# Values stationary in attention's PV, two heads in the column halves, and an order that fills gaps, in a four-branch mixer layer on one core

## The chip, the core and the metric

The kernel runs on one core of one Trainium2 chip. Times are device microseconds (us) of that core. The kernel before has a median of 295.15 us over 3 runs (294.05 to 296.47); one further execution was taken with the profiler.

## What is computed

One layer of a sequence mixer on x (512 x 1024, f32). A single input projection `proj = x @ w_in` has 14 column groups of 256: queries, keys and values of two attentions (`qa ka va`, `qd kd vd`), the input of a state-space layer (`us`), three inputs of a gated recurrence (`qc fc ic`) and four gates (`g0` to `g3`). Four branches of width 256 follow:

```
ya = moba_attention(heads(qa), heads(ka), heads(va), rel_bias[:, :4])      # at this length: causal attention
yb = s5_mixer(us, ...)                                                      # state-space layer and GLU
yc = hgrn2_mixer(qc, fc, ic, lb)                                            # gated recurrence, in chunks of 64
yd = dilated_attention(heads(qd), heads(kd), heads(vd), rel_bias[:, 4:])    # causal, weighted by a multiplicity
y  = concatenate([ya, yb, yc, yd])
yg = y.reshape(..., 16, 64); yg = yg * rsqrt(mean(yg*yg) + eps)             # per 64 channels
y  = (yg * branch_gain * silu(gates)) @ w_out
x  = layer_norm(alpha * x + y) * ln_g + ln_b
```

Each attention has 4 heads of width 64; per head `softmax(q k^T / 8 + bias) v`. All is f32 accuracy: where f32 products go through the fast one-pass form (f32r), each factor is split into a high and a low part and three products are summed.

## The kernel before, in words

**Matmuls.** The projection is done per column group and half (`mm3`, line 291; `projections`, line 425): 8 pieces of the contraction by 3 products, each 128x128 weights against 512 moving columns (256 for the token-major groups `ic va vd`). The output projection (`omm`, line 1225) takes units (token tile i, column half c): 8 pieces k by 3 products of 512 columns. Six of the pieces are the partial part (`out_partial`), the last two need the second attention and are the final part (`out_final`). For the last unit alone the final part is cut into two runs of 256 columns, both into the one PSUM tile of the unit.

**Attention** goes by branch br (0 or 1), token tile i in the order 3, 2, 1, 0, and head. `attn_pair` (line 1111) computes the scores of two heads, one in rows 0 to 63 and one in rows 64 to 127 of the array (`sc`). `attn_head` (line 1125) adds the bias on DVE (`nl<-sc,TB`), takes the exponential on ACT, transposes the tile in pieces of 128x128 on PE (`pt<-ident,nl`), and copies it back (`pT<-pt`, on DVE for odd heads, on ACT for even ones). Then PV: for each key tile kt up to i, `po` (128 tokens x 64 columns) accumulates with P as the stationary operand and the values as the moving one, 64 columns at a time. After four heads `attn_norm` (line 1166) squares `po` on ACT (`sqa`), reduces on DVE, takes a power on POOL (`msa`), scales on DVE (`ya<-po,msa`), transposes on PE (`yt<-ident,ya`), applies gain and gate (`z`), and splits into `yh` and `yl`. One PSUM bank (tag `sm`) holds `po` until `ya` has been read from it.

**Recurrence.** `hgrn` (line 869) builds chunk scores in one diagonal step and three levels li = 0, 1, 2. A step is 32 f32 matmuls in quadrants of the array into four PSUM tiles of one bank each (`hs`, tags `sc` and `pt`); DVE merges them into `st`, by 8 multiplications with the identity for the diagonal, by 12 masked copies (`COPY_PREDICATED st<-cst,hs`) for a level.

**What sets the order.** All instructions come out of one planner (`Order`, line 128). Each part of the program is a generator that yields one operation, or a list of them for PE, or a wait. The planner holds a clock per engine, prices each operation by a table (`Op.cost`, line 57), and takes the first task by priority whose next operation may go: a PE operation only if what it needs is planned to be ready 1 us earlier, others if they do not leave the engine waiting. Buffers are counted as tokens (`sc` 2, `pt` 2, `pj` 3, `sm` 1, `raw` 4). Every engine then runs its instructions in the order that came out, and waits where a needed result is late. The input weights and the output weights pass through four `raw` buffers: a DMA brings a piece, ACT makes the high part (`woh<-wro`), DVE the low part (`wol<-wro,woh`), and this frees the buffer for the next DMA.

All records of compute instructions have line 207 of the kernel, in `trace`, so they are told apart by their tiles.

Of the kernel before, what the change touches and what calls it, by code (L numbers as in the profile page):

```python
# [11 lines left out]
F32 = mybir.dt.float32  # L12
# [21 lines left out]
NCP = 16  # L34
NW = 5
# [15 lines left out]
class Op:  # L51
# [5 lines left out]
    def cost(self):  # L57
# [6 lines left out]
        if e == "PE":  # L64
# [4 lines left out]
            if self.a[1].dtype == F32:  # L69
                if self.a[0].shape[0] == 64 and self.a[1].shape[0] == 64:  # L70
                    return (0.03 + n / 600) / 4
                return 2 * max(0.107, 0.013 + n / 1200)
            return 0.013 + n / 2400
        if e == "DVE":
# [8 lines left out]
            if f == "tensor_tensor_scan":  # L83
                return 0.42
            return 0.09 + m * 0.00107
# [41 lines left out]
class Order:  # L127
# [31 lines left out]

    def step(self, t):  # L160
# [20 lines left out]
        else:  # L181
# [62 lines left out]
def build(ctx: ExitStack, tc: tile.TileContext, xT, xN, w_in, w_out, ln_g, ln_b,  # L244
# [18 lines left out]
    def ps(nm, tag, shape=(128, 512)):  # L263
        return pp.tile(list(shape), F32, tag=tag, name=nm, bufs=dict(pj=NPJ, sm=4 - NPJ).get(tag, 2))
# [604 lines left out]
    def hgrn():  # L869
# [6 lines left out]
        def scores(pss, nm, shape, col):  # L876
            for a in range(2):
                for h in range(2):
                    pss[h, a] = ps(f"hs{nm}_{h}{a}", ("sc", "pt")[h], (128, 4, shape))
            ops = []  # L880
            for a in range(2):
                for c2 in range(4):
                    for h, cpar in ((0, 0), (1, 1), (0, 1), (1, 0)):
                        c = 2 * c2 + cpar
                        rh = slice(64 * h, 64 * h + 64)
                        d_, r = col(pss[h, a][64 * cpar:64 * cpar + 64, c2], rh, a, c)
# [3 lines left out]
        pss = {}  # L890
        yield Tok(sc=2, pt=2)
        yield from scores(pss, "d", 64, lambda d_, rh, a, c: (d_, qc[rh, a, 64 * c:64 * c + 64]))
        for h in range(2):
            for a in range(2):
                for q in range(2):
                    sl = slice(64 * q, 64 * q + 64)
                    yield V.tensor_tensor(st[h][sl, a], pss[h, a][sl],
                                          ident[sl, sl].unsqueeze(1).to_broadcast([64, 4, 64]), OP.mult)
# [14 lines left out]
        for li, m in enumerate((1, 4, 16)):  # L913
# [15 lines left out]
            pss = {}  # L929
# [12 lines left out]
            for h in range(2):  # L942
                for a in range(2):
                    dst = st[h][:, a].rearrange("p c (n s) -> p c n s", n=nn)
                    sr = pss[h, a].rearrange("p c (n s) -> p c n s", n=nn)
                    for d0, s0, n_, o_ in ((m, 0, 3, 0), (2 * m, 3 * m, 2, 48), (3 * m, 5 * m, 1, 80)):
                        mm = msk[:, li, o_:o_ + 16 * n_].rearrange("p (n s) -> p n s", n=nn)
                        yield V.copy_predicated(dst[:, :, :, d0:4 * m], mm.unsqueeze(1).to_broadcast([128, 4, nn, n_ * m]),
                                                sr[:, :, :, s0:s0 + n_ * m])
# [20 lines left out]
            tot = nt  # L970
        o.done("hgrn levels")
# [136 lines left out]
    SUM = small([128, 2, 4, 4], "ssum")  # L1108
# [304 lines left out]
```

## Time and profile before

| | |
|---|---|
| median of 3 runs | 295.15 us (294.05 to 296.47) |
| profiled execution | 296.08 us, of which the traced span is 294.3 us |
| PE busy | 282.3 us (96%) |
| DVE busy | 214.2 us (73%) |
| ACT busy | 140.1 us (48%) |
| POOL busy | 25.0 us (8%) |
| PE share of the chain that ended last | 82% |
| mean granted clock of TensorE | 0.991 |

The span runs from the first to the last instruction. A matmul's duration includes the way through the array, so that neighbouring records overlap; what one costs is the distance to the next start. An f32 matmul leaves two records, an f32r matmul and a transpose one each. The chain that ended last is followed back from the last instruction to whatever released it.

### The profile page before, as it was taken

What the parts mean: (1) busy time and instruction counts of PE and PEld (TensorE: products, weight loads), DVE (VectorE), ACT (ScalarE), POOL (GpSimd) and SP (SyncE); (2) the same over time, 40 slices, a digit from 0 to 9 for tenths busy, and PEclk for the clock granted to TensorE, in tenths of its full rate; (3) what the DMA queues carried; (4) which work ended last, traced back from release to release, by engine and by line L of the source; (5) the groups of instructions that cost most, each with busy time, mean ns of one, the idle gap of its engine ahead of it and who ended that gap; (6) DMA issues with size and microseconds to landing.
All of it is one profiled execution on the core that took longest, in us unless ns stands there. A gap on an engine that the chain in (4) does not pass through costs nothing.

```text
span 294.3 us, 5178 instructions
## 1 busy us (share of the span) xinstructions
PE 282.3 (96%) x1932; PEld 234.0 (80%) x1932; DVE 214.2 (73%) x529; ACT 140.1 (48%) x273; POOL 25.0 (8%) x30
## 2 busy tenths in 40 slices
PE   8999999999999999999999999999998999999980
PEld 3768789888899878688888898878987788888870
DVE  2876899999999699747976444566569844866655
ACT  4677561324443632178434796468677533111000
POOL 1100010000000001103001000100250011111201
PEclk9999999999999999999999999999999999999996
DMA  6956535513221999501211203542003880030011
GB/s 196 300 187 221 145 91 116 165 59 108 65 82 40 151 139 141 161 34 55 74 71 71 75 9 82 160 148 68 2 0 106 233 295 14 5 139 38 36 71 71
DMA packets 18741, 31.08 MB, mean 106 GB/s; under 512 B 2426, under 2 KB 5882, under 8 KB 18716
## 3 DMA queue, kind: packets, MB, share of 16 engines
q1 hardware_dynamic: 18716, 30.76, 37.6%
q8 instruction: 15, 0.25, 0.4%
q14 instruction: 10, 0.08, 0.1%
HBM read 27.27 MB, written 2.42 MB: 101 GB/s over the span
## 4 chain that ended last, share of the span: by engine, by line
PE 82%; DMA 7%; DVE 5%; ACT 2%; issue 2%; SPq 1%; DVEq 0%
PE pj_g L207 15%; PE out L207 14%; PE po L207 5%; PE pj_ic L207 4%; PE pj_va L207 4%; PE pj_qc L207 4%; DMA wro<-in_w_out_dram 4%; PE pj_ka L207 4%; PE pj_qa L207 4%; PE pj_us L207 4%; PE pj_vd L207 4%; PE sc L207 3%; PE pj_kd L207 3%; PE pt L207 2%; DMA wrus<-in_w_in_dram 2%; PE y L207 2%
## 5 line engine op out<-in xcount | busy, mean ns | idle before, releaser
L207 PE MATMUL pj_g<-xh,whg 128*128 128x512 f32 x64 | 26.3, 411 | 0.0
L207 PE MATMUL pj_g<-xh,wlg 128*128 128x512 f32 x64 | 25.0, 391 | 0.0
L207 PE MATMUL pj_g<-xl,whg 128*128 128x512 f32 x64 | 25.0, 390 | 0.0
L207 ACT ACT_TABLE_LOAD x18 | 23.1, 1283 | 1.0 <-PEq L1402 0.7
L207 ACT ACTIVATE nl<-nl,nm 128x512 f32<-128x512 f32 (+3 forms) x32 | 17.8, 557 | 8.3 <-DVE nm L207 8.2
L207 PE MATMUL out<-woh,yh 128*128 128x512 f32 x48 | 19.8, 413 | 0.0
L207 POOL TENSOR_TENSOR msa<-msa,mhalf 128x4 f32<-128x4 f32 x8 | 9.9, 1240 | 106.5 <-DVE msa L207 106.5
L207 PE MATMUL out<-woh,yl 128*128 128x512 f32 x48 | 18.9, 393 | 0.0
L207 ACT ACTIVATE whg<-wrg 128x512 fp32r<-128x512 f32 x16 | 10.1, 628 | 18.2 <-PE pj_g L207 12.3
L207 PE MATMUL out<-wol,yh 128*128 128x512 f32 x48 | 18.7, 390 | 0.0
L207 DVE TENSOR_TENSOR wlg<-wrg,whg 128x512 fp32r<-128x512 f32 x16 | 11.0, 686 | 8.4 <-ACT whg L207 8.3
L207 DVE CUSTOM_DVE_ANT_0 nl<-sc,TB 128x512 f32<-128x512 f32 (+3 forms) x32 | 15.0, 486 | 2.4 <-PE pt L207 1.6
L207 PEld LDWEIGHTS pj_g<-xh,whg 128*128 128x128 f32 x64 | 12.0, 188 | 3.7 <-issue 1.2
L207 ACT ACTIVATE yh<-z 128x256 fp32r<-128x256 f32 (+1 forms) x12 | 5.8, 487 | 18.0 <-DVE z L207 17.9
L207 PEld LDWEIGHTS pj_g<-xh,wlg 128*128 128x128 f32 x64 | 12.0, 188 | 2.7
L207 PE MATMUL pt<-ident,nl 128*128 128x128 f32 x80 | 13.4, 276 | 0.3 <-ACT pT L207 0.3
L207 PEld LDWEIGHTS pj_g<-xl,whg 128*128 128x128 f32 x64 | 12.0, 188 | 2.1
L207 DVE COPY_PREDICATED st<-cst,hs 128x192 f32<-128x192 int32 (+2 forms) x36 | 11.8, 354 | 0.7 <-PE hs L207 0.2
L207 DVE COPY pT<-pt 128x512 f32<-128x512 f32 (+3 forms) x16 | 7.7, 486 | 6.1 <-PE pt L207 6.0
L207 ACT ACTIVATE pT<-pt 128x512 f32<-128x512 f32 (+3 forms) x16 | 6.9, 430 | 10.1 <-PE pt L207 10.1
L207 PEld LDWEIGHTS pt<-ident,nl 128*128 128x128 f32 x80 | 9.8, 146 | 2.0 <-ACT pT L207 0.7
L207 PEld LDWEIGHTS po<-vd,pT 128*128 128x128 f32 x80 | 10.1, 191 | 1.6 <-DVE pT L207 0.6
(309 smaller groups left out, 829.0 us busy)
## 6 DMA issues: line engine op xcount, KB each, us to landing
wrg<-in_w_in_dram SPq DMA_DIRECT2D x16, 256.0 KB, 4.2
wro<-in_w_out_dram SPq DMA_DIRECT2D x16, 256.0 KB, 3.0
xr<-in_xT_dram SPq DMA_DIRECT2D x8, 256.0 KB, 4.5
TB<-scr SPq DMA_DIRECT2D x8, 256.0 KB, 10.6
xn<-in_xN_dram SPq DMA_DIRECT2D x4, 512.0 KB, 9.1
out_dram<-xn SPq DMA_DIRECT2D x7, 256.0 KB, 2.0
raw<-in_w_in_dram SPq DMA_DIRECT2D x8, 128.0 KB, 4.5
wrus<-in_w_in_dram SPq DMA_DIRECT2D x4, 256.0 KB, 5.0
```

The lines of the kernel that those rows point to most:

```text
L207: getattr(self.engines[op.eng], op.name)(*op.a, **op.k)
```

## The change

Six things are changed.

- PV has the values as the stationary operand (128 x 64) and P as the moving one (128 columns). The two heads of a pair write PSUM partitions 0 to 63 and 64 to 127, alternately. A pair's PV is a task of its own that starts when both P are there (`attn_pv`).
- The result is then channel-major. `attn_norm` copies it to SBUF on ACT, transposes it back on PE with two 128x128 transposes into the other half of the same bank, and goes on as before.
- The planner gets `earlier`: before it places an operation on ACT, DVE or POOL that would leave this engine waiting, it looks for another task's operation that fits into the gap. Attention's tasks get priority 6.5 (10 before; the output weights' splits have 8). The price table is changed for f32 matmuls with 64 output partitions and for masked copies.
- The recurrence's scores go into two tiles of two banks each, so that one DVE instruction merges what two did.
- The last unit of the output projection becomes two units of 256 columns each, with a PSUM tile each.
- The PSUM pool of the recurrence is closed after its levels, and the pool of `sc` and `pt` opened in its place.

```diff
+FIT = 0.5
@@ class Op: cost
+                if self.a[0].shape[0] == 64:
+                    return 0.013 + n / 1200
                 return 2 * max(0.107, 0.013 + n / 1200)
...
+            if f == "copy_predicated":
+                return 0.24 + m * 0.00095
             return 0.09 + m * 0.00107
@@ class Order
+    def earlier(self, t, e):
+        for t2 in self.tasks:
+            if t2 is t:
+                continue
+            while isinstance(self.fetch(t2), Wait) and all(n in self.events for n in t2["next"].names):
+                self.step(t2)
+            x = t2["next"]
+            x = x[0] if isinstance(x, list) else x
+            if isinstance(x, Op) and x.eng == e and max(t2["chain"], self.clk[e]) + FIT * x.cost() < t["chain"]:
+                return t2
+        return None
...
+            if e not in ("PE", "SP") and t["chain"] > self.clk[e] + 0.1:
+                t2 = self.earlier(t, e)
+                if t2 is not None:
+                    return self.step(t2)
@@ def hgrn
-            for a in range(2):
-                for h in range(2):
-                    pss[h, a] = ps(f"hs{nm}_{h}{a}", ("sc", "pt")[h], (128, 4, shape))
+            for h in range(2):
+                pss.append(four["hp"].tile([128, 2, 4, 128], F32, tag=f"hs{h}", name=f"hs{nm}_{h}", bufs=1))
...
-                for a in range(2):
-                    dst = st[h][:, a].rearrange("p c (n s) -> p c n s", n=nn)
...
+                dst = st[h].rearrange("p a c (n s) -> p (a c) n s", n=nn)
...
+                    yield V.copy_predicated(dst[:, :, :, d0:4 * m], mm.unsqueeze(1).to_broadcast([128, 8, nn, n_ * m]),
+                                            sr[:, :, :, s0:s0 + n_ * m])
@@ def attn_head
-        yield [T.matmul(po[0][:, 64 * hd:64 * hd + 64], p_[:, kt], vt[v_][:, kt, 64 * hd:64 * hd + 64],
-                        start=(kt == 0), stop=(kt == i)) for kt in range(i + 1)]
+    def attn_pv(br, i, pairs):
...
+        yield [T.matmul(po[64 * h:64 * h + 64, a], vt[v_][:, kt, 128 * a + 64 * h:128 * a + 64 * h + 64],
+                        ATT[br, i, 2 * a + h][:, kt], start=(kt == 0), stop=(kt == i))
+               for a in pairs for kt in range(i + 1) for h in range(2)]
@@ def attn_norm
-        pg = po.rearrange("p (g c) -> p g c", c=64)
+        oT = y.rearrange("p (a t) -> p a t", a=2)
+        yield A.activation(oT, po[:, 0:2], AF.Copy)
+        yield [T.transpose(po[:, 2 + a], oT[:, a], ident) for a in range(2)]
+        pg = po[:, 2:4].rearrange("p a (g c) -> p (a g) c", c=64)
@@ output projection
-    UNITS = [(i, c) for i in TILES for c in range(2)]
+    UNITS = [(i, 512 * c, 512 * c + 512) for i in TILES for c in range(2)]
+    UNITS[-1:] = [(TILES[-1], 512, 768), (TILES[-1], 768, 1024)]
...
-            for cols in (slice(0, 512),) if (i, c) != LAST else (slice(0, 256), slice(256, 512)):
-                yield omm(i, c, KORD[6:8], cols)
-                o.add(out_evac(i, c, cols), 2, f"out {i} {c}")
+            yield omm(u_, KORD[6:8])
+            o.add(out_evac(*u_), 2, f"out {u_[0]} {u_[1]}")
```

The planner's order moves many instructions; three places matter below.

PE, the first token tile (i = 3) of the first attention. Before, the first two of its four heads:

```order
L207 MATMUL pj_g_1576<-xh_134,wlg_3_1567 128x512
L207 MATMUL pt_3_1711<-ident,nl_3_1636 128x128 x4
L207 MATMUL po_0_1721<-va,pT_0_1620 128x64 x4
L207 MATMUL po_0_1721<-va,pT_2_1709 128x64 x4
L207 MATMUL pj_g_1647<-xh_129,whg_2_1499 128x512
```

and with the change the end of its second pair and the transposes back:

```order
L229 MATMUL po_0_1785<-pT_2_1793,va 64x128
L229 MATMUL po_0_1785<-pT_3_1871,va 64x128
L229 MATMUL pt_1_1878<-ident,nl_1_1773 128x128 x3
...
L229 MATMUL pt_2_1925<-ident,nl_2_1837 128x128 x3
...
L229 MATMUL sc_1_1947<-ka_857,qa_1041 128x256
L229 MATMUL po_0_1785<-ident,ya_1915 128x128 x2
L229 MATMUL pj_kd_1964<-xh_122,whkd_1759 128x512
```

A head's four matmuls in a run have become eight that alternate between the pair's heads, and the transposes back stand behind a `pt` group, six projection matmuls, another `pt` group and six score matmuls.

DVE, where the output projection begins (`wol`: low part of the output weights; `COPY pT_7`: P of head 7 in the second attention's first token tile, needed by its PV). Before:

```order
L207 TENSOR_TENSOR wol_2561<-wro_1_2564,woh_2560 128x512
L207 TENSOR_TENSOR wol_2567<-wro_0_2574,woh_2566 128x512
L207 SCALAR_TENSOR_TENSOR z_1_2634<-yt_1_2604,cst,g2t 128x512
L207 TENSOR_TENSOR wol_2567<-wro_1_2591,woh_2566 128x512
L207 ISA nl_6_2643,nm_6_2644<-sc_6_2617,TB 128x384
L207 ISA nm_6_2644 128x1
L207 TENSOR_TENSOR yl_2519<-z_1_2634,yh_2518 128x512
L207 TENSOR_TENSOR wol_2598<-wro_0_2612,woh_2597 128x512
L207 TENSOR_TENSOR wol_2598<-wro_1_2621,woh_2597 128x512
L207 COPY pT_7_2668<-pt_7_2623 128x512
```

and with the change:

```order
L229 TENSOR_TENSOR wol_2437<-wro_0_2438,woh_2436 128x512
L229 COPY pT_7_2600<-pt_7_2559 128x512
L229 TENSOR_TENSOR wol_2437<-wro_1_2462,woh_2436 128x512
L229 TENSOR_TENSOR wol_2466<-wro_0_2552,woh_2465 128x512
L229 TENSOR_TENSOR wol_2466<-wro_1_2582,woh_2465 128x512
L229 TENSOR_TENSOR wol_2607<-wro_0_2608,woh_2606 128x512
L229 TENSOR_TENSOR wol_2607<-wro_1_2624,woh_2606 128x512
L229 TENSOR_REDUCE msa_2649<-sqa_2648 128x4
```

The copy of P has moved from behind the twelfth `wol` to ahead of the eighth; the second state-space branch's `z` and `yl` have left this stretch for an earlier one.

PE, the end of the program. Before, the last partial matmul of unit (0, 1) and its final part in two runs of six:

```order
L207 MATMUL out_1_3136<-woh_2597,yl_1901 128x512
L207 MATMUL out_1_3136<-who_1_2630,yh_2736 128x256
L207 MATMUL out_1_3136<-wlo_1_2632,yh_2736 128x256
L207 MATMUL out_1_3136<-who_1_2630,yl_2737 128x256
L207 MATMUL out_1_3136<-who_1_2657,yh_2736 128x256
L207 MATMUL out_1_3136<-wlo_1_2659,yh_2736 128x256
L207 MATMUL out_1_3136<-who_1_2657,yl_2737 128x256
```

and with the change the end of columns 512 to 767 and, in a tile of its own, the beginning of 768 to 1023, of which 24 matmuls follow to the end:

```order
L229 MATMUL out_512_3137<-who_1_2660,yh_2717 128x256
L229 MATMUL out_512_3137<-wlo_1_2662,yh_2717 128x256
L229 MATMUL out_512_3137<-who_1_2660,yl_2718 128x256
L229 MATMUL out_768_3166<-woh_2092,yh_1729 128x256
L229 MATMUL out_768_3166<-wol_2093,yh_1729 128x256
```

All 24 matmuls of the last 256 columns now stand behind the last matmul of the 256 before them.

## Rows read from the trace of the kernel before

**Rows 1.** The page's first part: busy time, share of the span, instructions of each engine.
```profile
PE 282.3 (96%) x1932; PEld 234.0 (80%) x1932; DVE 214.2 (73%) x529; ACT 140.1 (48%) x273; POOL 25.0 (8%) x30
```
**Rows 2.** Busy time by stretch: stretch, length, PE, PEld, DVE, ACT, POOL, clock, DMA.
```profile
160.00:180.00 20.00, 20.00 (x131) 17.44 (x131) 8.76 (x21) 16.54 (x28) 1.01 (x1) 1.00 0.18 50
220.00:240.00 20.00, 18.21 (x118) 15.20 (x116) 16.07 (x37) 12.96 (x28) 2.27 (x2) 1.00 0.64 192
```
**Rows 3.** Waits of PE, without the start: us in total, times, longest us.
```profile
PE yt L207 <- DVE z L207: 0.8, 1, 0.8
...
PE po L207 <- DVE pT L207: 0.4, 1, 0.4
PE pt L207 <- ACT pT L207: 0.3, 1, 0.3
PE yt L207 <- DVE ya L207: 0.2, 1, 0.2
PE po L207 <- ACT vd L207: 0.2, 1, 0.2
```
**Rows 4.** Chain that ended last, in order of time: start us, us, what.
```profile
19.03 10.90 PE pj_us L207 x48
...
144.32 1.73 PE po L207 x16
...
211.06 0.22 PE yt L207 x2
...
212.23 1.44 PE pj_vd L207 x12
```
**Rows 5.** PE by form, first attention's PV; the second's is alike (vd).
```profile
L207 PE MATMUL po<-va,pT 128*128 128x64 f32 x80 | 10.2, 269 | 0.0
```
**Rows 6.** PE in order of time, recurrence's output: start us, duration us, instruction, count.
```profile
129.26 0.39 PE L207 MATMUL pj_g<-xh,wlg 128*128 128x512 f32 x1
129.58 1.09 PE L207 MATMUL ho<-hst,qc 128*64 128x128 f32 x16
130.60 1.15 PE L207 MATMUL ho<-ic,st 64*64 64x64 f32 x32
```
**Rows 7.** PE in order of time, around one group of scores.
```profile
121.74 0.39 PE L207 MATMUL pj_g<-xh,wlg 128*128 128x512 f32 x1
122.06 0.96 PE L207 MATMUL sc<-ka,qa 64*128 64x512 f32 x6
122.95 0.50 PE L207 MATMUL pj_g<-xh,whg 128*128 128x512 f32 x1
123.29 0.40 PE L207 MATMUL pj_g<-xl,whg 128*128 128x512 f32 x1
```
**Rows 8.** DVE by form, masked copies of the recurrence.
```profile
L207 DVE COPY_PREDICATED st<-cst,hs 128x192 f32<-128x192 int32 x12 | 5.0, 420 | 0.2 <-PE hs L207 0.2
L207 DVE COPY_PREDICATED st<-cst,hs 128x64 f32<-128x64 int32 x12 | 3.6, 298 | 0.3
```
**Rows 9.** All engines in order of time at the end of the output projection.
```profile
285.15 0.28 PE L207 MATMUL out<-who,yl 128*128 128x256 f32 x1
...
285.87 0.28 PE L207 MATMUL out<-who,yl 128*128 128x256 f32 x1
286.19 0.42 DVE L207 SCALAR_TENSOR_TENSOR xn<-xn,out 128x256 f32<-128x256 f32 x1 [1.31 <-PE out L207]
...
286.99 0.40 DVE L207 SCALAR_TENSOR_TENSOR xn<-xn,out 128x256 f32<-128x256 f32 x1
...
287.88 0.26 DVE L207 BATCH_NORM_AGGREGATE mv<-bst 128x2 f32<-128x24 f32 x1
```
**Rows 10.** The chain again, where output weights are loaded.
```profile
226.87 3.81 DMA wro<-in_w_out_dram
230.70 0.64 ACT woh L207
```
**Rows 11.** ACT in order of time, the square behind a PV.
```profile
218.16 0.38 ACT L207 ACTIVATE sqa<-po 128x256 f32<-128x256 f32 x1 [0.47 <-PE po L207]
```

More of the change, by code (lines that the diff above doesn't have):

```diff
@@ L263, in ps @@
     def ps(nm, tag, shape=(128, 512)):
-        return pp.tile(list(shape), F32, tag=tag, name=nm, bufs=dict(pj=NPJ, sm=4 - NPJ).get(tag, 2))
+        return (pp if tag in ("pj", "sm") else four["sp"]).tile(
+            list(shape), F32, tag=tag, name=nm, bufs=dict(pj=NPJ, sm=4 - NPJ).get(tag, 2))
+    levels = ExitStack()
+    four = dict(hp=levels.enter_context(tc.tile_pool(name="hp", bufs=1, space=PSUM)))
     def small(shape, nm, dt=F32):
@@ L893, in hgrn @@
         for h in range(2):
-            for a in range(2):
[L895 to L898, printed above, removed]
+            for q in range(2):
+                sl = slice(64 * q, 64 * q + 64)
+                yield V.tensor_tensor(st[h][sl], pss[h][sl, :, :, 0:64],
+                                      ident[sl, sl].unsqueeze(1).unsqueeze(1).to_broadcast([64, 2, 4, 64]), OP.mult)
             o.rel(("sc", "pt")[h], 2)
@@ L970, in hgrn @@
             tot = nt
+        levels.close()
+        four["sp"] = ctx.enter_context(tc.tile_pool(name="sp", bufs=2, space=PSUM))
         o.done("hgrn levels")
@@ L1108, in build @@
     SUM = small([128, 2, 4, 4], "ssum")
+    PVH = 2
+    HP = 6.5
     ATT = {}
@@ L1212, in attention @@
                     yield Tok(head=2)
-                    o.add(attn_pair(br, i, a, n), 10 + n * 0.01, f"pair {br} {i} {a}")
+                    o.add(attn_pair(br, i, a, n), HP + n * 0.01, f"pair {br} {i} {a}")
                     n += 2
@@ L1230, in omm @@
             for a_, b_ in ((yh_, woh), (yh_, wol), (yl_, woh)):
-                ops.append(T.matmul(pos[i, c][:, cols], a_, b_[k][c][:, cols], start=(k == KORD[0] and a_ is yh_ and b_ is woh),
-                                    stop=(k == KORD[-1] and a_ is yl_ and cols.stop == 512)))
+                ops.append(T.matmul(pos[u_][:, 0:hi - lo], a_, b_[k][lo // 512][:, cols],
+                                    start=(k == KORD[0] and a_ is yh_ and b_ is woh),
+                                    stop=(k == KORD[-1] and a_ is yl_)))
         return ops
@@ L1236, in out_partial @@
         yield Wait("proj", ("z", 3), ("z", 2))
-        for i, c in UNITS:
+        for u_ in UNITS:
             yield Tok(pj=1)
-            pos[i, c] = ps(f"out{i}_{c}", "pj")
+            pos[u_] = ps(f"out{u_[0]}_{u_[1]}", "pj")
             for j in range(0, 6, 2):
@@ L1268, in build, with out_evac @@
     sts = {}
-    def out_evac(i, c, cols):
+    def out_evac(i, lo, hi):
         yield Wait("ln", ("xn", i))
         xr = xr_[i]
-        lo, n = 512 * c + cols.start, cols.stop - cols.start
-        end = lo + n == D
-        parts = 4 if i == LAST[0] else 2
+        parts = 4 if i == TILES[-1] else 2
         if lo == 0:
@@ L1282, in out_evac @@
         st = sts[i]
-        cs = slice(lo, lo + n)
-        yield V.scalar_tensor_tensor(xr[:, cs], xr[:, cs], ALPHA, pos[i, c][:, cols], OP.mult, OP.add)
-        if cols.stop == 512:
-            o.rel("pj")
+        cs = slice(lo, hi)
+        yield V.scalar_tensor_tensor(xr[:, cs], xr[:, cs], ALPHA, pos[i, lo, hi][:, 0:hi - lo], OP.mult, OP.add)
+        o.rel("pj")
         w = D // parts
-        for a in range(lo, lo + n, w):
+        for a in range(lo, hi, w):
             yield V.bn_stats(st[:, a // w], xr[:, a:a + w])
-        if not end:
-            o.done(("columns", i, lo + n))
+        if hi < D:
+            o.done(("columns", i, hi))
             return
```

57 lines of the change are left out of this document (30 added, 27 removed).

## The prediction, made before the changed kernel had run

> **What bounds the kernel now.** I read the page's first part, then busy time by stretch, then what PE waits for, then the chain of waits, and last PE and DVE record by record at the places that the change touches. TensorE is busy for 282.3 us, 96% of the span [rows 1]; in 160 to 180 us it is busy for 20.00 of 20, and the other stretches from 40 us on read alike up to 180, while in 220 to 240 it loses 1.8 us [rows 2]. After the start its waits make up only 1.9 us, all between 194 and 233 us: 0.8 for a `z` of the state-space layer, 0.4 and 0.3 for P, 0.2 for `ya`, 0.2 for the values [rows 3]. So PE sets the end, and time moves in three ways only: PE has less to do, one of these waits goes or comes, or the tail behind the last matmul gets shorter. Time saved on another engine is worth nothing unless PE waits for that engine.
>
> All sums are against the profiled execution's 296.08 us (span 294.3); the median of the runs shown is 0.93 lower.
>
> **Prices.** Records overlap, so I take distances between starts. A stretch of the chain gives 0.108 us per PV record (1.73 for 16), 0.227 per 512-column f32r record (10.90 for 48), 0.12 per 256-column one (1.44 for 12), 0.11 per transpose (0.22 for 2) [rows 4]. What a change of array form costs is seen at the recurrence's output, whose instruction has just the new PV's form, 128 rows by 64 columns and 128 moving columns: `pj_g` starts at 129.26 and should hold PE for 0.23, the 16 `ho` records start at 129.58, 0.09 later than that, and the next form follows 1.02 after it [rows 6]. The scores, in row halves, tell the rest: 0.09 in, and 0.89 us until the next `pj_g`, of which three pairs side by side need 3 x 0.227 = 0.68, so 0.21 out; the first f32r matmul behind f32 ones then takes 0.34 rather than 0.23 [rows 7]. I take 0.30 per stretch of a tiled form, and 0.11 for each return to f32r.
>
> **A. PV.** Before, 80 records for each attention [rows 5], 160 x 0.108 = 17.3 us. With values stationary there are as many records at the same duration, but neighbours lie in different column halves. The `ho` stretch bears the pairing out: 8 x 0.108 = 0.86 and a switch of 0.16 make the 1.02 that 16 records took [rows 6]. That gives 8.65 us. The order has 15 stretches of the new form (16 pairs, two adjoining), 15 x 0.30 = 4.5. In all 13.15, a saving of 4.1 us. Bounds: 8.65 if a switch were free, 21.8 if nothing overlaps; I take the middle value since both its parts come from rows of the nearest form.
>
> **B. Transposes back.** 8 tiles of two, 16 x 0.11 = +1.8 us on PE. The copy ahead of them is ACT's: the same 128 x 256 from PSUM took 0.38 [rows 11], 8 x 0.38 = 3.0 us, on an engine busy for 16.5 of 20 us at its fullest [rows 2]. What hides it is the PE work between the last PV and the transposes, in the order's matmuls 1.7 to 3.0 us; the round trip needs about 0.6 (0.38 and the ends of two queues, an estimate). If that cover were gone, 0.6 us per tile would be a wait of PE. I take 0.
>
> **C. More changes of form.** f32r matmuls stand in 67 stretches against 56 in the order before: 11 x 0.11 = +1.2 us.
>
> **D. Last unit as two.** Its 18 partial matmuls of 512 columns become 36 of 256: 36 x 0.12 - 18 x 0.23 = +0.2 us.
>
> A to D together: -4.1 + 1.8 + 1.2 + 0.2 = **-0.9 us** of PE work.
>
> **E. The tail.** Before, the first half's final matmuls were issued by 285.15 and the last by 285.87, but DVE's first evacuation waited 1.31 us and began only at 286.19, behind the last matmul of all, since both halves lie in one tile [rows 9]. It evacuates 256 columns, then at 286.99 the other 256. With a tile each the first pair runs while the 24 matmuls behind it (24 x 0.12 = 2.9 us) go on, and only one pair is left: 286.99 - 286.19 = **-0.8 us**. Bounds 0 and -0.8.
>
> **F. The waits.** The bounds are -1.9, all of them gone, and 0, as much new wait as old. The state-space branch's `z` and `yl` are issued earlier, which takes the 0.8. The copy of P for the last head stands ahead of the eighth `wol`, not behind the twelfth; a `wol` is as late as the 3.81 us of its weights' DMA and the 0.64 us of their high part [rows 10], so the PV behind it no longer waits for the loads (0.4). The rest is near its neighbour's time either way. What is late next is a `wol`: four in a row now stand behind the copy, and the last is to be had some 4.5 us later. DVE will idle there, while PE holds 32 PV records, a transpose group, scores and six output matmuls, above 4 us in sum. I take **-1.4 us**.
>
> **Hidden, at nothing.** The two-bank tiles make one masked copy of two. Two sizes give its price, 420 ns for 192 and 298 for 64 elements, so 0.95 ns per element and 237 ns fixed [rows 8]; 18 copies fewer are 18 x 0.237 = 4.3 us less of DVE, and the diagonal's multiplications save an estimated 0.6 more. PE is full in these stretches, so it is worth 0. A single bank fewer is no loss while the scores of the next level find the tile read: in the order they stand behind 24 matmuls of `ka`, 5 us. Without that cover each level could cost a copy's 0.6 us.
>
> Sum: -0.9 - 0.8 - 1.4 = -3.1. From 296.08 that is 293.0, and with the median's 0.93 less **292.0 us**, 1.1% below before.
>
> **The rivals.**
>
> *Forecast* (0.60): as above. Its own range takes A's switches at 0.21 to 0.39 (1.4 either way) and F between -1.9 and -0.8: 290.5 to 293.5, of which a little over half lies under 292.2, 1% below before. One per cent, up or down, is about what a measurement of this kernel can tell from no change.
>
> *The gain is eaten* (0.22). The waits move rather than go (F = 0), and switches and returns cost what the scores' whole stretch shows, 0.41, so 15 x 0.11 = 1.7 more. For: the transposes back and their form changes are certain while overlap is an inference from one row. Against: the copies that PE waited for do stand earlier. 292.0 + 1.4 + up to 1.7 = 293.4 to 295.
>
> *A full halving* (0.05). Halves run side by side with no price of switching, and nothing is lost in more f32r stretches. PV goes from 17.3 to 8.65, and the sum is -8.65 + 1.8 + 0.2 - 0.8 = -7.5 with the waits left: 287.6. Against: the 1.02 us of 16 `ho` records contains 0.16 of switch [rows 6]. The Trainium skill names just this step, "TensorEngine Tiling (Array Packing)", sections "Theoretical Speedup" and "Performance Considerations": where the moving operand is at most 64 wide, swap stationary and moving and tile the columns, for up to twice the speed; PV was 64 wide here. Its "Key Properties" say that a change of tiling mode drains the array, which speaks against the whole halving in 15 short stretches, and the 0.30 per stretch agrees with it.
>
> *Slower, by the new round trip* (0.09). Between PV and normalisation PE now waits for ACT, and ACT for PE. ACT's queue is in order, and at 83% busy at its fullest [rows 2] an exponential whose `nm` comes late from DVE stands ahead of the copy. Then PE reaches the transposes before the copy is done, and behind them wait the projections. It decides where ACT is over 1.1 us late at the thinnest cover (1.7 less 0.6). The bank `sm` is single, so the next tile's PV waits as well, until `ya` has been read. If it happened at all 8 tiles, with 0.6 to 1.0 us each, +4.8 to +8 on 292.0: 296.8 to 300. Against: PE's wait for `ya`, the same sort of round trip over three engines, was 0.2 us in all [rows 3].
>
> *Slower, no overlap* (0.04). If the two halves did not run side by side, PV would take 21.8, and 292.0 + 8.65 = 300.6. That is the case in which the change does not do what it says. From some 40% of pairs without overlap on it is slower than before (3.1 of 8.65). Against: 16 `ho` records in 1.02, which without overlap would have been 1.73.
>
> **Range and chances.** The range must leave out no more than 2 in 10. Below 289.3 lies the halving and a sliver of the forecast; above 295.9 both slower cases. In between lie nearly all of the forecast and of the eaten gain, 0.60 + 0.22 and a little less: 289.3 to 295.9. Faster by over 1%: somewhat more than half of the forecast and the halving, 0.37 + 0.05 = 0.42. Slower by over 1% (above 298.1): most of the slower cases, 0.11, and 0.02 for mishaps of the order that I did not see, 0.13. Within 1%: 0.45.
>
> **What would show it.** A: in the chain or in PE's records by time, a stretch of 16 `po` records takes 1.0 to 1.2 us to the next form's start, not 1.73; near 2 us would make it the no-overlap case, 0.86 the halving. B: 16 transposes `po<-ident,ya` or alike, with no wait of PE for ACT behind `po`; a row of PE waiting for that copy, above 2 us in sum, would make it the round trip. C: PE's busy time falls to about 281. E: between the last matmul and the aggregate of the statistics there is one pair of DVE evacuations, and the first pair is done before. F: PE's waits after the start fall under 0.8 us and none names `z`. The two-bank tiles: 18 masked copies at about 600, 480 and 360 ns, with DVE's busy time some 5 us lower and PE untouched by it. The forecast is wrong if the waits behind the four late `wol` reach PE's output matmuls, or if a stretch of the new form costs far more or less than 0.30 on top of its pairs.

## The result, and the profile after

The changed kernel takes 292.14 us (median of 4 runs, 290.89 to 292.68); runs of the kernel before on the same chip gave 295.81 (294.05 to 296.88). The ratio is 0.9882, 95% interval [0.9847, 0.9918]. The forecast was 292.0. The profiled execution took 292.68 us, its span is 290.9.

The first part of its page, which answers to [rows 1] (busy time, share of the span, instructions):

```profile
PE 279.9 (96%) x1966; PEld 225.8 (78%) x1966; DVE 211.3 (73%) x507; ACT 142.6 (49%) x281; POOL 23.5 (8%) x30
```

PE has 2.4 us less to do, DVE 2.9 less, ACT 2.5 more, mostly the eight copies of PV's result (0.38 each). What PE waits for after the start, against [rows 3] (us in total, times, longest):

```profile
PE vri L229 <- DVE s5ta L229: 1.3, 1, 1.3
...
PE hs L229 <- DVE qbt L229: 0.5, 1, 0.5
```

All five waits of [rows 3] are gone, and none names the new copy on ACT. Two others stand in their place, both earlier in the program: the state-space layer's matmuls and the recurrence's scores. PE in order of time, at the first transposes of P, two of the new PV stretches and the next instruction behind each (start us, duration us, instruction, count):

```profile
131.07 0.60 PE L229 MATMUL pt<-ident,nl 128*128 128x128 f32 x4
131.42 0.48 PE L229 MATMUL pj_g<-xh,whg 128*128 128x512 f32 x1
131.74 0.39 PE L229 MATMUL pj_g<-xl,whg 128*128 128x512 f32 x1
...
157.09 1.09 PE L229 MATMUL po<-pT,va 128*64 128x128 f32 x16
158.11 0.50 PE L229 MATMUL pj_g<-xh,whg 128*128 128x512 f32 x1
...
182.52 0.88 PE L229 MATMUL po<-pT,va 128*64 128x128 f32 x12
183.32 0.44 PE L229 MATMUL pt<-ident,nl 128*128 128x128 f32 x2
```

16 PV records hold PE for 1.02 us, not the 1.73 of [rows 4]; 12 for 0.80. The two stretches differ by 0.22 for 4 records, some 0.054 each, which is half of before's 0.108, and leave 0.16 per stretch. The upper rows price the return from transposes to f32r: four transposes take 0.35, 0.09 less than 4 x 0.11, and the f32r matmul behind them 0.32, 0.09 more than usual. Together they cost nothing extra.

The end, DVE in order of time; the last matmul starts at 283.25 (compare [rows 9]):

```profile
281.91 0.41 DVE L229 SCALAR_TENSOR_TENSOR xn<-xn,out 128x256 f32<-128x256 f32 x1
...
283.57 0.42 DVE L229 SCALAR_TENSOR_TENSOR xn<-xn,out 128x256 f32<-128x256 f32 x1 [0.79 <-PE out L229]
...
284.49 0.27 DVE L229 BATCH_NORM_AGGREGATE mv<-bst 128x2 f32<-128x24 f32 x1
```

One evacuation is left behind the last matmul; the aggregate follows that matmul's start by 1.24 us, where it was 2.01.

To compare kernels I split each profiled span into four parts that add up to it: the **start** (first record of `pj_us`), from there to the end of the last matmul the **waits** of PE and the rest, PE's **work**, and the **tail** behind it. For the span of before that is 18.9 + 1.9 + 265.4 + 8.1 = 294.3, for the changed kernel 18.5 + 1.8 + 263.3 + 7.4, before rounding 290.9.

| kernel | median us (runs) | ratio to before, 95% | start | work | waits | tail |
|---|---|---|---|---|---|---|
| before | 295.81 (4) | | 18.9 | 265.4 | 1.9 | 8.1 |
| changed | 292.14 (4) | 0.9882 [0.9847, 0.9918] | 18.5 | 263.3 | 1.8 | 7.4 |
| changed, again | 292.52 (6) | 0.9884 [0.9841, 0.9927] | 19.2 | 263.3 | 0.9 | 7.4 |
| old PV | 292.97 (6) | 0.9889 [0.9851, 0.9928] | 17.8 | 265.3 | 0.5 | 7.3 |
| halves apart | 294.24 (12) | 0.9940 [0.9910, 0.9970] | 18.0 | 265.9 | 1.0 | 7.4 |
| no gap filling | 295.20 (12) | 0.9972 [0.9938, 1.0006] | 19.0 | 263.2 | 5.2 | 7.4 |
| last unit as one | 292.02 (6) | 0.9851 [0.9804, 0.9898] | 17.9 | 263.0 | 0.9 | 8.1 |
| one-bank tiles | 291.09 (6) | 0.9849 [0.9814, 0.9885] | 18.6 | 262.3 | 1.4 | 7.3 |
| only the new PV | 297.39 (12) | 1.0039 [1.0011, 1.0068] | 18.9 | 265.4* | 4.4 | 8.2 |
| late price | 294.03 (12) | 0.9938 [0.9907, 0.9968] | 18.9 | 264.5* | 2.7 | 7.4 |
| four heads in one | 297.33 (12) | 1.0044 [1.0019, 1.0070] | 18.8 | 264.2* | 4.5 | 8.1 |
| priority 10 | 291.92 (6) | 0.9867 [0.9824, 0.9910] | 18.1 | 262.9 | 1.2 | 7.4 |
| order only | 293.11 (6) | 0.9899 [0.9861, 0.9937] | 17.7 | 265.0 | 0.7 | 7.4 |
| small tiles merged | 293.01 (8) | 0.9890 [0.9851, 0.9929] | 19.0 | 263.3* | 2.6 | 7.4 |

The starred works hold a stretch in which TensorE's granted clock was half, 6.8 us of it in "only the new PV" and 3.4 in the other three; at most half of that is lost time (below). The start differs by up to 1.5 us between kernels whose order is the same up to there, so it belongs to the first loads, not to the edits. Works and waits are from one execution each, medians from all. Most edits let the planner make a new order from some point on, so that two kernels in the table can differ by more than the edit names; on PE only the halves apart and the changed kernel again have the changed kernel's order from end to end, and the last unit as one has it up to 276 us.

### The profile page after: what moved, and what is told of

Read it like the earlier page. It is cut to its first block, busy times and chain, and to the rows that moved or that the text cites. A ratio compares the mean times of both kernels' runs of the same rounds, so it can differ in the third digit from the quotient of the medians.

```text
span 290.9 us, 5251 instructions
## 1 busy us (share of the span) xinstructions
PE 279.9 (96%) x1966; PEld 225.8 (78%) x1966; DVE 211.3 (73%) x507; ACT 142.6 (49%) x281; POOL 23.5 (8%) x30
## 4 chain that ended last, share of the span: by engine, by line
PE 84%; DMA 7%; DVE 5%; issue 1%; SPq 1%; ACT 1%; DVEq 0%; ACTq 0%
PE out L229 16%; PE pj_g L229 12%; PE po L229 4%; PE pj_vd L229 4%; PE pj_ic L229 4%; PE pj_kd L229 4%; PE pj_va L229 4%; PE pj_qc L229 4%; PE pj_qd L229 4%; PE pj_ka L229 4%; PE pj_us L229 4%; DMA wrg<-in_w_in_dram 4%; PE pt L229 3%; PE sc L229 3%; PE pj_qa L229 2%; PE y L229 2%
## 5 line engine op out<-in xcount | busy, mean ns | idle before, releaser
L229 PE MATMUL pj_g<-xh,whg 128*128 128x512 f32 x64 | 26.9, 421 | 0.0
L229 PE MATMUL out<-woh,yh 128*128 128x512 f32 (+1 forms) x54 | 21.1, 391 | 0.0
L229 ACT ACTIVATE nl<-nl,nm 128x512 f32<-128x512 f32 (+3 forms) x32 | 17.8, 556 | 6.3 <-DVE nm L229 6.1
L229 PE MATMUL out<-woh,yl 128*128 128x512 f32 (+1 forms) x54 | 19.9, 368 | 0.0
L229 PE MATMUL out<-wol,yh 128*128 128x512 f32 (+1 forms) x54 | 19.8, 367 | 0.0
L229 POOL TENSOR_TENSOR msa<-msa,mhalf 128x4 f32<-128x4 f32 x8 | 9.0, 1122 | 100.8 <-DVE msa L229 100.8
L229 ACT ACTIVATE yh<-z 128x256 fp32r<-128x256 f32 (+1 forms) x12 | 5.7, 486 | 18.8 <-DVE z L229 18.8
L229 PE MATMUL pt<-ident,nl 128*128 128x128 f32 x80 | 14.3, 278 | 0.0
L229 PEld LDWEIGHTS out<-woh,yh 128*128 128x128 f32 x54 | 10.2, 190 | 2.4 <-issue 0.8
L229 PEld LDWEIGHTS out<-woh,yl 128*128 128x128 f32 x54 | 10.2, 189 | 1.8
```

What stands on the lines that cost most here:

```text
L229: getattr(self.engines[op.eng], op.name)(*op.a, **op.k)
```

## The experiments

**Old PV in the changed kernel** (e1). Is the new form what saves PE's time?

```diff
-        yield [T.matmul(po[64 * h:64 * h + 64, a], vt[v_][:, kt, ...], ATT[br, i, 2 * a + h][:, kt], ...)
-               for a in pairs for kt in range(i + 1) for h in range(2)]
+        yield [T.matmul(po[:, 128 * a + 64 * h:...], ATT[br, i, 2 * a + h][:, kt], vt[v_][:, kt, ...], ...)
+               for a in pairs for h in range(2) for kt in range(i + 1)]
...
-        yield A.activation(oT, po[:, 0:2], AF.Copy)
-        yield [T.transpose(po[:, 2 + a], oT[:, a], ident) for a in range(2)]
```

> The changed kernel, but PV again with P stationary (160 records), without the copy on ACT and the two transposes back; the planner's gap filling, priorities, two-bank tiles and the last unit as two stay. Terms as forecast (PV -4.1, transposes +1.8, changes of form +1.2): PE work up by 1.1 us, time 293.2. As I now read the changed kernel's trace (PV -5.2, transposes +1.8, changes of form +0.5): PE work up by 2.9 us, 295.0, if the waits stay at 1.8. Rival, that PV's form is worth nothing and the rest of the change made the gain: 292.1.

Work is 265.3, 2.0 above the changed kernel: midway between the two sums. But the median rises only to 292.97, 0.8 above one set of runs of the changed kernel and 0.5 above the other, and by the ratios to before the difference is 0.2. In this profile the wait of 1.3 for the state-space product did not occur. The third theory, that the form is worth nothing, is refuted for PE's work; of the time, the form's share here is less than the intervals (1.1 us either way) can tell from nothing. The order is the changed kernel's up to the first PV only, and another from there on.

**Halves apart** (e5). Do records overlap because they lie in different column halves?

```diff
-               for a in pairs for kt in range(i + 1) for h in range(2)]
+               for a in pairs for h in range(2) for kt in range(i + 1)]
```

> The changed kernel, but in each pair's PV all matmuls of head 0 (column half 0 to 63) come first, then all of head 1, rather than alternately; nothing else moves. If neighbouring records overlap only where they lie in different halves, which is what the gain in PV rests on: a stretch of 16 records takes 1.73 + 0.16 rather than 1.02, all 160 records 8.65 us more, less one overlap per stretch, time about 300. Rival, that the records are short whatever half they are in (the moving operand's form, not the side-by-side halves): PV unchanged, 292.1.

Neither came out. PE in order of time, stretches of 16, 12 and 8 records with what follows, and last the 8 records of the changed kernel:

```profile
155.75 1.58 PE L229 MATMUL po<-pT,va 128*64 128x128 f32 x16
157.26 0.50 PE L229 MATMUL pj_g<-xh,whg 128*128 128x512 f32 x1
...
182.43 1.15 PE L229 MATMUL po<-pT,va 128*64 128x128 f32 x12
183.51 0.44 PE L229 MATMUL pt<-ident,nl 128*128 128x128 f32 x2
...
192.98 0.66 PE L229 MATMUL po<-pT,va 128*64 128x128 f32 x8
193.58 0.44 PE L229 MATMUL pt<-ident,nl 128*128 128x128 f32 x2
...
192.82 0.66 PE L229 MATMUL po<-pT,va 128*64 128x128 f32 x8
193.41 0.44 PE L229 MATMUL pt<-ident,nl 128*128 128x128 f32 x2
```

16 records take 1.51, 12 take 1.08, and 8 take 0.60, as long as alternating ones (0.59). Less the 0.16 of a stretch, at 0.108 a record, they last as long as 12.5, 8.5 and 4.1 records one after the other. So it is as if about four records (3.5 to 4) of the second half ran beside the end of the first. Up to 8 records in a stretch the order of the halves was free; at 12 and 16 alternating was faster. That records in different halves overlap is shown, since only their order was changed; the reach of about four is worked out from these three lengths, and it is why the cost was 2.7 us of PV, not 8.65. With the halves apart the new form is no gain at all: work 265.9, with the old PV 265.3.

**No gap filling** (e2).

```diff
-            if e not in ("PE", "SP") and t["chain"] > self.clk[e] + 0.1:
+            if False:
```

> The changed kernel with the planner's search for earlier work off; its prices and attention's priority of 6.5 stay. Every order after the first microseconds changes. If the gap filling took away what PE waited for before, as forecast: waits of PE about 1.4 us above the changed kernel's 1.8, time 293.5. If it only moved the waits, as the changed kernel's trace suggests (1.8 against 1.9): within 0.7 us of 292.1, with other waits of 1 to 2.5 us in sum.

Work is the same (263.2), the waits are 5.2 rather than 0.9 to 1.8, and the time is 295.20, more than the higher theory said. What PE waits for:

```profile
PE pj_vd L229 <- ACT whvd L229: 2.2, 2, 1.2
...
PE po L229 <- DVE pT L229: 0.8, 2, 0.4
PE pj_vd L229 <- DVE wlvd L229: 0.7, 2, 0.3
PE yt L229 <- DVE ya L229: 0.6, 1, 0.6
PE pt L229 <- ACT pT L229: 0.6, 1, 0.6
```

The waits for P and `ya` are of the kinds of [rows 3], more and longer; the largest, 2.9 us for the weights of the second attention's values (`whvd`, `wlvd`), are new. Without gap filling the faster PV comes with waits, here and in "only the new PV" below, in two different orders.

**Last unit as one** (e3).

```diff
-    UNITS[-1:] = [(TILES[-1], 512, 768), (TILES[-1], 768, 1024)]
...
+            for cols in (slice(0, 512),) if u_ != UNITS[-1] else (slice(0, 256), slice(256, 512)):
```

> The changed kernel with the last unit of the output projection as one PSUM tile, its final part in two runs, as before; the order ahead of it stays. As forecast: the span behind the last matmul longer by 0.8 us (one more DVE evacuation behind the last matmul), PE work shorter by 0.2 to 0.5: time 292.4 to 292.7. Rival, that the tail is set by something else (POOL's power, the last output DMA): 291.6 to 292.0, the second half's evacuation hidden anyway.

The tail is 8.1 rather than 7.4 (8.11 against 7.37), the work 0.2 less: both as forecast. The median, 292.02, does not show the half microsecond, which is under what its runs scatter (290.47 to 293.17).

**One-bank tiles in the recurrence** (e4).

```diff
-                pss.append(four["hp"].tile([128, 2, 4, 128], F32, tag=f"hs{h}", ...))
+                    pss[h, a] = ps(f"hs{nm}_{h}{a}", ("sc", "pt")[h], (128, 4, shape))
```

> The changed kernel with the recurrence's scores in four tiles of one bank, four multiplications more and 18 masked copies more on DVE, as before; everything else as changed. As forecast, the 4.9 us of DVE work are beside a full PE and worth 0: time 292.1, DVE busy 216 us. If the single two-bank tiles brought the 0.5 us wait of the scores for qbt and moved the first state-space matmuls' wait of 1.3, the old tiles give some of it back: 290.8 to 291.6. If DVE was what PE waits for in the recurrence: 293 to 295.

291.09: the 3.2 us of DVE work that come back (busy 214.5) cost nothing that shows, and no gain of the two-bank tiles is seen. The kernel may even be faster, but its interval overlaps the changed kernel's. It is the fastest of all that ran. The run does not separate the tiles from the order, though: from 60 us on its order is another, with 13 stretches of PV in place of 15 and 57 of f32r matmuls in place of 67, and its work is 1.0 us less.

**Only the new PV, on the kernel before** (e6). The mirror image of the first experiment; the edit is the diff's PV part without the rest.

```diff
+    PVH = 2
+    HP = 10
...
-        if hd == 0:
-            yield Tok(sm=1)
-            ATT[br, i] = [ps(f"po{i}_{br}", "sm", (128, W)), 0]
+        ATT[br, i, hd] = p_
+        o.done(("P", br, i, hd))
+        if hd % PVH == PVH - 1:
+            o.add(attn_pv(br, i, range((hd + 1 - PVH) // 2, (hd + 1) // 2)), HP + no * 0.01, f"PV {br} {i} {hd}")
```

> The kernel before with only the new PV (values stationary, pairs, copy on ACT, transposes back, and the price of the new form); priority 10, no gap filling, one-bank tiles, last unit as one. Terms as forecast: PE work -1.1 us against before, 294.7. As I now read the changed kernel's trace: PE work -2.9, so 292.9 if the waits stay at about 1.9. The rival of a new round trip between PE and ACT, which the gap filling and the priority may have hidden: waits of PE on the copy of 0.6 to 1 us at each of 8 tiles, 297 to 301.

It is slower than before, by 0.4% [0.1, 0.7], and not through the round trip: no wait names the copy. PE in order of time, with the idle time before an instruction and its releaser in brackets:

```profile
224.16 0.41 PE L209 MATMUL yt<-ident,ya 128*128 128x128 f32 x2 [0.68 <-DVE ya L209]
224.50 0.43 PE L209 MATMUL po<-pT,vd 128*64 128x128 f32 x2
226.99 1.97 PE L209 MATMUL po<-pT,vd 128*64 128x128 f32 x14 [2.06 <-DVE pT L209]
228.89 0.79 PE L209 MATMUL out<-woh,yh 128*128 128x512 f32 x1
229.48 0.63 PE L209 MATMUL out<-wol,yh 128*128 128x512 f32 x1
```

DVE in the same microseconds:

```profile
223.59 0.42 DVE L209 TENSOR_TENSOR ya<-po,msa 128x256 f32<-128x256 f32 x1 [0.90 <-POOL msa L209]
223.93 1.89 DVE L209 TENSOR_TENSOR wol<-wro,woh 128x512 fp32r<-128x512 f32 x3
225.74 0.60 DVE L209 SCALAR_TENSOR_TENSOR z<-yt,cst,g0t 128x128 f32<-128x128 f32 x2
226.25 0.68 DVE L209 COPY pT<-pt 128x512 f32<-128x512 f32 x1
```

And busy time by stretch (stretch, length, PE, PEld, DVE, ACT, POOL, granted clock, DMA):

```profile
222.00:226.00 4.00, 1.86 (x8) 0.69 (x6) 3.10 (x8) 1.54 (x3) 1.32 (x1) 1.00 0.62 179
226.00:230.00 4.00, 3.01 (x17) 2.49 (x18) 3.18 (x7) 2.57 (x5) 0.00 (x0) 0.52 0.73 243
230.00:234.00 4.00, 4.00 (x13) 3.13 (x12) 3.17 (x7) 2.75 (x7) 0.00 (x0) 0.63 0.78 244
```

Three `wol` and two `z`, 2.3 us, stand ahead of the copy of P that PE needs, and PE is idle for 2.06. Within this wait TensorE's clock falls to its lower level, 1.2 GHz: the output's 512-column records last 0.63, not 0.39, and this goes on for 6.8 us by the granted clock. For the first 0.8 of them PE is still idle; of the other 6.0 half is lost, about 3.0 us of work: more than the wait itself. All 12 executions of this kernel have a mean granted clock under 0.990 (0.979 to 0.989), where the changed kernel's profiles have 0.994 and 0.991.

**Late price** (e7). Was the 1.3 us wait in the changed kernel DVE's order behind a late load?

```diff
-            o.events["raw", p] = o.cur["chain"]
+            o.events["raw", p] = o.cur["chain"] + (10.0 if "hgrn levels" in o.events
+                                                   and o.clk["PE"] < o.events.get("TB", 1e9) + 2.0 else 0)
```

> The changed kernel, where the planner takes the input weights that are loaded while the bias table is coming in to land 10 us later than its price says (the trace shows 10.8 us for one such load, the price says 2 to 3). DVE's low part of the weights then stands behind the state-space products that PE waited for. If that in-order wait was the 1.3 us: it goes, PE's waits fall to about 0.5 and the time to 290.8, unless the new order brings others of the same size. If the late load delays PE anyway (its weights are what the projection lacks): a wait of PE on the low part in place of it, 292.1.

The place in the changed kernel, DVE in order of time:

```profile
118.35 0.69 DVE L229 TENSOR_TENSOR wlg<-wrg,whg 128x512 fp32r<-128x512 f32 x1
119.91 0.61 DVE L229 SCALAR_TENSOR_TENSOR hst<-hst,tot,pu 128x128 f32<-128x128 f32 x2 [0.87 <-PE pu L229]
125.38 0.69 DVE L229 TENSOR_TENSOR wlg<-wrg,whg 128x512 fp32r<-128x512 f32 x1 [4.86 <-ACT whg L229]
125.99 0.42 DVE L229 TENSOR_TENSOR z_r<-vri,tr 128x256 f32<-128x256 f32 x1
126.32 0.41 DVE L229 TENSOR_TENSOR z_i<-vri,ti 128x256 f32<-128x256 f32 x1
126.65 0.41 DVE L229 TENSOR_TENSOR s5ta<-vri,ti 128x256 f32<-128x256 f32 x1
```

and what this `wlg` hangs on, ACT's high part of the same weights and the load of these weights, issued at 110.24 (size, us to landing):

```profile
124.71 0.63 ACT L229 ACTIVATE whg<-wrg 128x512 fp32r<-128x512 f32 x1 [6.39 <-DMA wrg<-in_w_in_dram]
...
wrg<-in_w_in_dram SPq DMA_DIRECT2D x1, 256.0 KB, 14.4
```

DVE sits 4.86 us behind one `wlg`, whose weights were 14.4 us in transit behind the bias table's loads, with four products behind it whose matmuls had started at 121.30. (The 10.8 us of the expectation are those of a later load of the same kind, issued at 115.18.) With the late price they run at 122.74, and the wait is gone, as expected. The time is not mended: 294.03. The planner changed everything behind this place, and in the profiled execution PE waits 1.3 us for an exponential at a later transpose, 0.6 for `ya`, and has 3.4 us at half clock; the eight of the 12 executions with a mean clock of 0.992 or more still take 293.9 in the median. So the cause of that wait is shown, and that mending it in this way is no gain. One price made later moved the time by 1.5 to 1.9 us, so a difference of that size between two orders need not come from what the edit was meant to do. In the seven profiles with the same order up to there, the wait was 1.3, 0.9, 0.7, 0.5, 0.4, 0.2 and none: how late the load is differs from run to run.

**Four heads in one stretch** (e8), and **small tiles merged** (e11, on the one-bank kernel).

```diff
-    PVH = 2
+    PVH = 4
```
```diff
-        if hd % PVH == PVH - 1:
+        pvh = 4 if i < 2 else PVH
+        if hd % pvh == pvh - 1:
```

> The changed kernel with the PV of all four heads of a token tile in one stretch: 8 stretches in place of 15. At 0.25 us a stretch (0.10 in, 0.16 out) and 0.1 for the f32r matmul behind it, 7 stretches fewer give -1.8 to -2.5 us of PE work: 289.7 to 290.4. Rival: PV waits for the last head of four, so that P's buffers and the tile's bank are held longer; PE's waits or ACT's copies come late, and the gain is lost: 292 to 295.

> The one-bank kernel (291.1), with the PV of all four heads in one stretch for the two small token tiles only (i = 1 and 0): 10 stretches of the new form in place of 13. At 0.25 us a stretch: 0.75 us less PE work, 290.3. If the wait for the last of four heads costs here too, as it did with all tiles merged (waits 4.5 us, and a stretch at half the clock): 291.5 to 293.

Both rivals came true, the first beyond its range (297.33, for 292 to 295), the second at its edge (293.01, for 291.5 to 293). PE's waits with all merged:

```profile
PE sc L229 <- DVE nm L229: 1.3, 2, 1.1
...
PE out L229 <- ACT yh L229: 1.2, 1, 1.2
...
PE vri L229 <- DVE s5ta L229: 0.9, 1, 0.9
PE hs L229 <- DVE qbt L229: 0.8, 2, 0.5
PE po L229 <- DVE pT L229: 0.4, 1, 0.4
```

and with the small tiles merged:

```profile
PE yt L229 <- DVE ya L229: 2.2, 1, 2.2
```

The stretches do get cheaper (32 records in 1.90, 0.14 less than two of 16), but PV waits for four heads and the order behind it is another. With all merged the profiled span is 4.8 us above the changed kernel's: 2.7 of it are waits, 1.0 work (with a stretch at half clock), 0.7 the tail, 0.4 the start. The clock is not what makes it slow, since the six executions with a mean clock of 0.990 and more are no faster (297.4 in the median). With the small tiles merged it plays a part: the three of eight executions with 0.992 or more take 291.1 to 292.1. In both, work saved on PE by delaying an operation was paid back in waits; which of the waits come from the merging and which from the new order was not tried.

**Priority 10** (e9), **order only** (e10: the one-bank kernel with old PV) and the **changed kernel again**, side by side.

```diff
-    HP = 6.5
+    HP = 10
```

> The changed kernel with attention's priority back at 10; the gap filling stays. Without gap filling the changed kernel took 295.2, PE's waits 5.2 us. If the gap filling alone takes the waits away: 292, waits under 2 us. If it needs the priority, so that the output weights' splits stand behind attention's copies: waits of PE for P or ya of 2 us and more between 194 and 233 us, 294 to 295.

> Gap filling, prices, priority and the last unit as two, but PV with P stationary and the recurrence's scores in one-bank tiles: the change of order alone, on the kernel before. If the order makes nearly all of the gain, as old PV (293.0) beside the changed kernel (292.1) suggests: 292 to 293, waits under 1.5 us. If PV's saving is real time, 2.0 us of PE work by the traces: the same as the one-bank kernel plus 2.0, 293.1. If old PV and old tiles both undone bring the waits of before back: 295 to 296.

> The changed kernel once more, beside the other three on one chip, as their standard: 292.1, with PE's wait for the state-space product anywhere between 0 and 1.3 us (in four kernels with the same order up to there it was 0, 0.2, 0.5 and 1.3).

291.92, 293.11 and 292.52. The priority is worth nothing beside the gap filling. The order, without the new PV and the two-bank tiles, takes 2.8 of the 3.4 us by which the changed kernel beats before on this chip; 0.7 of it is the last unit's shorter tail, and its waits are 0.7 against before's 1.9. The 293.11 is also just what the second theory gave, the one-bank kernel plus 2.0. PE's waits in the changed kernel here:

```profile
PE hs L229 <- DVE qbt L229: 0.5, 1, 0.5
PE vri L229 <- DVE s5ta L229: 0.4, 1, 0.4
```

The order-only kernel has only the first of the two, at 0.7, with the same tile and releaser.

## Why the prediction was right, point by point

The sum was right (-3.1 forecast, -3.4 between the profiled executions, -3.7 between the medians). A and C came out better than forecast by 1.1 and 0.7 us, F worse by 0.3 to 1.2, and one coupling was not seen. That the total is so close is partly luck. Between the two profiled executions PE's work fell by 2.1, 1.2 more than forecast, the waits by 0.2, 1.2 less than forecast, and these two misses cancel; the tail came out as forecast, and the remaining 0.4 is the start, which no edit touched.

- **A, PV.** Forecast -4.1. The records went from 17.35 to 11.01 us in 15 stretches, plus 0.10 for each change into the new form that does not show there (14 found, 1.3): -5.2 with the 0.2 that before spent in the same way. The mis-sized term is the price of a stretch: 0.30 was taken from the scores' row halves, the column halves cost 0.10 in and 0.16 out, the figures that [rows 6] showed for this very form. Over 15 stretches this is 0.8 of the 1.1 us; the rest is the 0.2 that the sum left out and rounding. The Trainium skill, "TensorEngine Tiling (Array Packing)", "Key Properties", says that a change of tiling mode drains the array. The trace agrees, with a cost of 0.26 us for each stretch here.
- **B, transposes back.** +1.8 forecast, 1.6 to 1.8 measured, and no wait for the copy in any kernel that ran with it. The cover held.
- **C, changes of form.** +1.2 forecast, 0.3 to 0.5 measured: a return to f32r from transposes costs nothing, since the transposes ahead of it end sooner by the same 0.09; only a return from tiled forms and from PV costs (by the first f32r matmuls behind them 3.1 us in all before, 3.4 after). A to C sum to about -3, forecast -1.1. The whole work fell by 2.1 against before and stands 2.0 under the old PV's; with D's +0.2, some 0.6 to 0.8 us lie in small differences of other matmuls that I did not assign.
- **D and E.** +0.2 and -0.8; the experiment with the last unit as one gave 0.2 and -0.7. Right.
- **F, the waits.** -1.4 forecast; -0.2 in the changed kernel's first profile, -1.1 in its second. All five waits that were named went, and none names `z`, but the sign "under 0.8 us" was missed in both profiles (1.8 and 0.9). What failed is the step "what is late next is a `wol`": next came the recurrence's scores, whose query blocks DVE makes behind a `wlva` (0.5; the `wlva` takes 0.6, but that it is the cause was not tried), and the state-space product behind the late `wlg` (0 to 1.3), both in stretches that were called full.
- **Hidden, at nothing.** The two-bank tiles show no gain in time, as forecast. Their DVE saving was about 2.9 us in the copies, not 4.3: a copy of 384, 256 and 128 elements takes 642, 544 and 445 ns, so the fixed part of these copies is 0.35 rather than the 0.24 of [rows 8]. It is the form that got dearer, not only the fit that was off: a copy of 128 elements took 345 ns in the one-bank tiles.

DVE by form in the changed kernel, for that last point, and last the copy of 128 elements in the kernel before:

```profile
L229 DVE COPY_PREDICATED st<-cst,hs 128x384 f32<-128x384 int32 x6 | 3.9, 642 | 0.4 <-PE hs L229 0.3
L229 DVE COPY_PREDICATED st<-cst,hs 128x256 f32<-128x256 int32 x6 | 3.3, 544 | 0.1
...
L229 DVE COPY_PREDICATED st<-cst,hs 128x128 f32<-128x128 int32 x6 | 2.7, 445 | 0.1
...
L207 DVE COPY_PREDICATED st<-cst,hs 128x128 f32<-128x128 int32 x12 | 4.1, 345 | 0.2
```

What the sum did not see is that A to C and F are not independent. Alone, the new PV makes the kernel slower by 1.2 us (waits 4.4 us, half clock); the order with the shorter tail makes it 2.8 faster; all together 3.4 to 3.7, and with one-bank tiles, which the first two have as well, 4.5 to 5.1. PE's 2.0 us of work saved is time only where the other engines' orders keep up: PE's waits are 0.9 to 1.8 us in the changed kernel, but 2.6 to 4.5 in three kernels that have gap filling too (late price and the two with merged heads). The forecast took the waits of before as the base of F, but the base was the 4.4 to 5.2 us of the two kernels that have the new PV without gap filling. That this is the gap filling's doing rests on three orders (5.2 us without it and 0.9 to 1.8 with it, 4.4 on the kernel before); gap filling alone, on the kernel before with nothing else changed, was not tried.

Of the rivals, the gain eaten (293.4 to 295) is near what happens without gap filling (295.20), but through more waits than it supposed (5.2 us, not 1.9) and not through dearer switches. The full halving was excluded by the 0.26 per stretch. Of the slower ones, no overlap was refuted by the 1.02 us of 16 records and by the experiment with the halves apart, and the round trip did not occur. Of the two slower kernels that did occur, "only the new PV" lost its time to DVE's queue ahead of P and to the clock; "four heads in one" lost it to waits of several kinds.

Open: how much time the new PV is worth on top of the order. By records it is 2.0 us with two-bank tiles and 2.7 with one-bank tiles; the medians give 0.5 to 0.8 with two-bank tiles (by the ratios to before 0.2), and 2.0 with one-bank tiles, where the two kernels ran at different times (by their ratios to before 1.5). Each of these ratios is uncertain by 1.1 us or so. Open too is whether the one-bank kernel is faster than the changed one. And whether the gap filling shortens the start was not tried.

## What to carry to other kernels

Before crediting a saving on the busiest engine, ask which orders the other engines' queues were in when it was slower: here the saving came with waits until the queues were reordered, and the reordering with the shorter tail gave most of the gain. Where a planner makes the order, one small edit gives another order and can move the time by as much as what is being measured. Two operands' halves that share the array pay only if the halves alternate or the runs are short (up to 8 records here); a stretch of its own form costs a fixed sum, but merging stretches by making work wait cost more than it saved. Price a switch from the nearest form in the trace, not from a neighbour of it.

## What the hardware showed that was not expected

- A wait of PE can cost more than its length. In "only the new PV" PE was idle for 0.68 and then 2.06 us between 223 and 227, and then the granted clock was 0.52 and 0.63 of full speed in the next two stretches of 4 us; 512-column records went from a distance of 0.23 to 0.43. The profiles of the other three starred kernels have the same with 3.4 us, the changed kernel's have none. The kernel before loses clock in some executions too, though its profile shows no such stretch: 17 of the 65 that ran beside the experiments have a mean granted clock of 0.979 to 0.988, a mean that among the profiles only those with a stretch at half clock have, and these take 1.1 to 2.2 us longer on average than the rest. Of the changed kernel's 10 executions one has it (0.988, 294.51 us). So part of the gain, some 0.3 to 0.8 us by the medians with and without these executions, is clock that before loses at times, and the forecast had no term for it.
- Records of the other column half overlap about four records at the end of a run in one half (8 records: 0.59 alternating and 0.60 in runs; 16: 1.02 and 1.51).
- A single 256 KB load took 14.4 us from issue to landing when the bias table's last loads had been issued ahead of it; the median of its kind in that kernel is 4.9.
